# A decoder block in float32 on Trainium2: one tile of a depthwise convolution from TensorE to VectorE, another from VectorE to GpSimd

## The chip, the cores and the metric

The kernel runs on one core of one Trainium2 chip. The metric is the device time of one launch, in microseconds. Five engines take part, each with an instruction queue of its own that it works through in order: TensorE (PE, matmuls), VectorE (DVE), ScalarE (ACT), GpSimd (POOL), and SyncE (SP), which issues the loads and stores.

## The reference

One block with batch 1, 256 tokens, width 2048, all in float32. The convolution is depthwise and causal with 31 taps: each of the 2048 channels has its own taps.

```python
mod = silu(c) @ mod_w + mod_b                       # six vectors of 2048
h = rms_norm(x, norm1_g) * (1 + sc1) + sh1
u = h @ conv_w_in + conv_b_in                       # 2048 -> 4096
a, gt = split(u, 2);  u = a * sigmoid(gt)
u = depthwise_conv(u, conv_dw_w, 31 taps) + conv_dw_b
y = silu(layer_norm(u, ln_g, ln_b)) @ conv_w_out + conv_b_out
x = x + (1 + g1) * y
h = rms_norm(x, norm2_g) * (1 + sc2) + sh2
x = x + (1 + g2) * (square(relu(h @ mlp_w1)) @ mlp_w2)
```

## The kernel before

Activations lie with channels on the 128 partitions: 16 tiles of 128 channels by 256 tokens. The weights are loaded once, one megabyte at a time (128 by 2048), into seven buffers named `raw`.

A float32 product is made of three products of shorter numbers. For each weight block two halves of 128x1024 are prepared. ScalarE copies the **high part** (`hi`, L206), and another engine subtracts it from the weight to get the **low part** (`lo`, L209). Both have six buffers. In the input jobs GpSimd makes the low parts; later it makes some, VectorE the others.

The work is a list of jobs. Job n from 0 to 15 gives tile n of the gated input (`u`): it multiplies h by two weight blocks, one for `a`, one for the gate. Jobs 0 to 7 are done together at the start, while the modulation columns are loaded. Jobs 8 to 15 follow one at a time (`mm`, L234 and L235; in job 15 L230 to L232), then eight output jobs (`out`), then the jobs of the MLP (`up`, `down`).

In the loop over jobs, step n first splits the weights of job n+1 (`splits`), so GpSimd works one job ahead of TensorE. Then come the matmuls of job n, the evacuation (L532, L533) and the gate (L798, L800) that write `u[n]`.

The convolution of the 16 tiles is shared between two engines:

- On **TensorE**, the tiles of `PE_TILES` (`pe_conv`, L783): 32 matmuls with small diagonal blocks. Each tile needs a `diag` of its taps, made by GpSimd (L768), and a `wide` copy of `u`, 16 copies of 32x284 (`copy_wide`, L758 on VectorE and L760 on ScalarE). `CONV_AT` says behind which job's matmuls a tile stands, `COPY_AT` in which step ScalarE makes its copies.
- On **VectorE**, the others (`conv_steps`): one instruction of 128x256 per tap (L666 to L672), sums in PSUM (`acc`), two tiles interleaved. `ADVANCE` says how many taps are issued in step n.

Tile 0 and tile 1 come first, because a shift (an estimate of the mean, `find_shift`, L718) is taken from them. It is added to all tiles ahead of the statistics of the layer norm: tiles below `UNSHIFTED` = 7 get it later (`add_shift`), the others while they are summed.

Between jobs TensorE also multiplies 32 **row chunks** of `mod_w` (`mod_chunk`, L324), four matmuls each. `LATE_IN[n]` says how many follow job n. When a group of 16 is complete, ScalarE copies the sums (`rowsb`, L331) and TensorE folds them (L371). `stats` (L728) sums tiles and squares for the layer norm.

In an output job ScalarE scales the result in two halves (L1006), VectorE adds x (L1007), and the weights of the next job are split meanwhile (L206, L209).

The Tile framework's scheduler puts all this into one order per engine. `tc.issue_after(x)` makes an instruction stand behind x in that order, and `urgent()` raises its priority. The order is fixed when the kernel is built.

Of the kernel before, what the change touches and what calls it, by code (L numbers as in the profile page):

```python
# [8 lines left out]
F32 = mybir.dt.float32  # L9
F32R = mybir.dt.float32r  # L10
AF = mybir.ActivationFunctionType
ALU = mybir.AluOpType
PSUM = bass.MemoryType.PSUM

P = 128
T = 256
D = 2048
KT = D // P
FF = 4 * D
QUARTERS = FF // D  # L20
TAPS = 31
# [18 lines left out]
COLS += [w * KT + k for w in (SH2, G2) for k in range(KT)]  # L40
RAW = 7
FIRST = 4
PE_TILES = (0, 1, 2, 9, 10, 12, 14, 15)
CONV_AT = {9: (0,), 10: (1,), 11: (2,), 12: (9,), 13: (10,), 14: (12,), 15: (14,)}
ADVANCE = {7: 41, 8: 14, 9: 46, 10: 46, 11: 39, 12: 31, 13: 27, 14: 99}
SHIFT = 2
COPY_AT = {8: 0, 9: 1, 10: 2, 11: 9, 12: 10, 13: 12}
PADDING = 720
UNSHIFTED = 7
LATE_IN = [0] * 8 + [4, 4, 4, 4, 4, 2, 0, 10]  # L50
AHEAD = 2
LATE_OUT = [1, 1, 2, 3, 3, 3, 1, 1]
COLS_IN = 1
# [13 lines left out]
def conv_block(ctx: ExitStack, tc: tile.TileContext, x, vec, dwq, c_row, mod_r, mod_c, w_first, w_in, w_out, w1, w2, out):  # L67
    nc = tc.nc
# [12 lines left out]
    nc.scalar.dma_start(v[:, 0:soon], vec[:, 0:soon])  # L81
    dwq_sb = const.tile([P, 32 * len(PE_TILES)], F32, name="dwq_sb")

    def col(name, j=0, n=1):
        at = VEC[name] + j
        return v[:, at : at + n]
# [31 lines left out]
    state = {"used": 0}  # L118
# [12 lines left out]
    def urgent():  # L131
        return tc.high_priority(offset=URGENT)
# [56 lines left out]
    def take(key):  # L189
        assert order[state["used"]] == key, (order[state["used"]], key)  # L190
        state["used"] += 1
        waiting[home(key)] -= 1
        top_up()
        return raw.pop(key)

    def split_w(key, engine):
        w = take(key)
        if key[:2] == ("up", 0) and key[2] < UNSCALED:
            shown[key] = w
        halves = []  # L200
        for h in range(2):
            ks = slice(h * HALF, (h + 1) * HALF)
            hi = wts.tile([P, HALF, P], F32R, name="hi", bufs=6)
            lo = wts.tile([P, HALF, P], F32R, name="lo", bufs=6)
            with tc.issue_after(state["silu"]) if key == ("out", 1, 1) else ExitStack():
                state["w_hi"] = nc.scalar.activation(hi, w[:, ks, :], AF.Copy).ins  # L206
            by = nc.vector if key == ("in", HELD, 0) and h == 0 else engine
            with tc.issue_after(state["e_end"]) if key[0] == "out" and engine is nc.vector else ExitStack():
                end = by.tensor_tensor(lo, w[:, ks, :], hi.bitcast(F32), op=ALU.subtract)  # L209
            if by is nc.gpsimd:  # L210
                state["pool"] = end.ins
            halves.append((hi, lo))
        parts[key] = halves
# [8 lines left out]
    def mm(p, c, key, acts_of, ks=range(KT), merged=False):  # L222
        halves = parts[key]
        for k in ks:
            hi, lo = halves[k // HALF]
            m = acts_of[k // 2][:, k % 2, :]
            if merged:
                out_p, begin, end = p[:, c, 0:T], k == 0, k == KT - 1
                w = hi[:, k % HALF, :]
                nc.tensor.matmul(out_p, w, m[:, 0:T], start=begin, stop=False)  # L230
                nc.tensor.matmul(out_p, w, m[:, T : 2 * T], start=False, stop=False)  # L231
                state["mm_end"] = nc.tensor.matmul(out_p, lo[:, k % HALF, :], m[:, 0:T], start=False, stop=end)  # L232
                continue
            nc.tensor.matmul(p[:, c, :], hi[:, k % HALF, :], m, start=(k == 0), stop=(k == KT - 1))  # L234
            state["mm_end"] = nc.tensor.matmul(  # L235
                p[:, c, T : 2 * T], lo[:, k % HALF, :], m[:, 0:T], start=False, stop=(k == KT - 1),
                skip_group_check=True,
            )
# [204 lines left out]
    def ps_two():  # L443
        return ps.tile([P, 2, T], F32, name="acc", bufs=2)

    def two():
        return tmp.tile([P, 2, T], F32, name="two", bufs=6)
# [40 lines left out]

    quota = {("in", i): n for i, n in enumerate(LATE_IN)}
    quota.update({("out", i): LATE_OUT[i] for i in range(HALF)})  # L490
    after = {}
    for job in jobs:
        n = quota.get(job, 0)
# [3 lines left out]
        if job[:2] in LATE_GATE:  # L497
            n = LATE_GATE[job[:2]][job[2]]
# [22 lines left out]
    def splits(job):  # L521
        for c in range(2):
            if job + (c,) in parts_early:
                continue
            on_pool = job[0] == "in" or job in POOLED
            with urgent():
                split_w(job + (c,), nc.gpsimd if on_pool else nc.vector)

    def evac(p, cs=slice(0, 2), out=None):
        t1 = two()[:, cs, :]  # L530
        t2 = two()[:, cs, :] if out is None else out
        nc.scalar.activation(t1, p[:, cs, T : 2 * T], AF.Copy)  # L532
        nc.vector.tensor_tensor(t2, p[:, cs, 0:T], t1, op=ALU.add)  # L533
        return t2
# [4 lines left out]
    for k2 in range(HALF):  # L539
        s = two()  # L540
# [8 lines left out]
    with urgent():  # L549
        part = two()[:, 0, :]  # L550
# [64 lines left out]
    for k in range(KT):  # L615
# [4 lines left out]
        if c == 0:  # L620
            n = two()
# [7 lines left out]
        if last:  # L629
            w = take(("first", k))  # L630
# [16 lines left out]
    cp = conv_pool.__enter__()  # L647
# [4 lines left out]
    def cv(k):  # L652
        return cvs[k // 4][:, k % 4, :]
# [6 lines left out]
    def tap_of(ct, j):  # L660
        return u[ct][:, j : j + T], col("dww", ct * TAPS + j)
# [21 lines left out]
            yield  # L683
        join(cv(ct), acc[:, 1, :], rest)

    on_dve = [ct for ct in range(KT) if ct not in PE_TILES]

    def stream():
        tail = iter(())
# [18 lines left out]
    def advance(n):  # L708
        for _ in range(n):
            next(conv_taps, None)  # L710
# [40 lines left out]
    def copy_wide(ct, both=True):  # L751
        wides[ct] = cp.tile([P, 4, T + 28], F32, name="wide", bufs=2)
        for q in range(4):
            for g in range(4):
                dst = wides[ct][32 * q : 32 * q + 32, g, :]
                src = u[ct][32 * g : 32 * g + 32, q : q + T + 28]
                if both and (g % 2 or (q, g) == (3, 2)):
                    nc.vector.tensor_copy(dst, src)  # L758
                else:
                    nc.scalar.activation(dst, src, AF.Copy)  # L760
# [3 lines left out]
    def make_diag(ct):  # L764
        diags[ct] = cp.tile([P, 32, 32], F32, name="diag", bufs=2)
        at = PE_TILES.index(ct)
        with tc.issue_after(state["pool"]):
            nc.gpsimd.tensor_tensor(  # L768
                diags[ct],
                col("same", 0, 32)[:, None, :].to_broadcast([P, 32, 32]),  # L770
                dwq_sb[:, 32 * at : 32 * at + 32][:, :, None].to_broadcast([P, 32, 32]),
                op=ALU.mult,
            )
# [22 lines left out]
    def gate(i, t2):  # L796
        sg = two()[:, 0, :]
        state["sg"] = nc.scalar.activation(sg, t2[:, 1, :], AF.Sigmoid, bias=col("b_in", KT + i))  # L798
        u[i] = ubufs[i % len(ubufs)]
        state["gated"] = nc.vector.scalar_tensor_tensor(  # L800
            u[i][:, PAD : PAD + T], t2[:, 0, :], col("b_in", i), sg, op0=ALU.add, op1=ALU.mult
        ).ins
        return sg
# [6 lines left out]
    with urgent():  # L810
        split_w(jobs[HELD] + (0,), nc.gpsimd)
        take(("vec", 0))
        with tc.issue_after(state["w_hi"]):
            gate(0, held[0])
        for i in range(1, 6):
            gate(i, held[i])
        with tc.issue_after(state["sg"].ins):
            split_w(jobs[HELD] + (1,), nc.gpsimd)
        with tc.issue_after(state["w_hi"]):
            gate(6, held[6])  # L820
        gate(7, held[7])
    advance(ADVANCE[HELD - 1])

    for n, job in enumerate(jobs):
        if n < HELD:
            continue
        for ct in CONV_AT.get(n, ()) + ((15,) if n == KT - 1 else ()):
            make_diag(ct)
        if n == KT - 1:
            taken = [(key, take(key)) for key in cols_in]  # L830
        if n < len(jobs) - 1:
            splits(jobs[n + 1])
        if n in COPY_AT:
            with tc.issue_after(state["sg"].ins) if n == HELD else ExitStack():
                copy_wide(COPY_AT[n], False)
        if n == KT - 1:
            for key in parts_early:
                split_w(key, nc.gpsimd)
        kind, i = job[0], job[-1]
# [25 lines left out]
        elif kind == "in":  # L865
            rows = [key for key in after[job] if key not in cols_in] if i < KT - 1 else []
            for c in range(2) if i < KT - 1 else (1, 0):
                for ks in (range(HALF), range(HALF, KT)):
                    with tc.issue_after(state.pop("rows_end")) if "rows_end" in state else ExitStack():
                        mm(p, c, job + (c,), hl, ks, i == KT - 1)  # L870
            if not CONV_AT.get(n):
                with tc.issue_after(state["mm_end"].ins):
# [8 lines left out]
        if kind == "in":  # L881
            with urgent():
                gate(i, evac(p, out=p[:, :, 0:T]) if i < KT - 1 else p[:, :, 0:T])
                if i >= KT - 2:
                    copy_wide(i)
            if n == KT - 4:
                add_shift(cvs[0], 4)
                add_shift(cvs[1][:, 0:3, :], 3)
# [2 lines left out]
            if n == KT - 1:  # L891
                state["e_end"] = add_shift(cvs[3][:, 0:1, :], 1)
                for key, w in taken:
                    mod_col(key[1], w)
            for ct in CONV_AT.get(n, ()):
                with tc.issue_after(state["mm_end"].ins):
# [7 lines left out]
            with tc.issue_after(state["gated"]):  # L904
                advance(ADVANCE.get(n, 0))
            if n == KT - 2:
# [51 lines left out]
            for k2 in range(HALF):  # L958
                e = two()
                if k2 == 0:  # L960
                    with urgent():
                        nc.gpsimd.tensor_tensor(e, pair_of(cvs, 0), spread(mu), op=ALU.subtract)
                        new_hl(0)
                        f = [ps_two()[:, 0, :] for _ in range(2)]
# [10 lines left out]
                f = ps_two()  # L975
# [93 lines left out]
        else:  # L1069
# [13 lines left out]
            for t, cs, p in sums.pop((kind, i // 2)):  # L1083
                at = slice(512 * (i // 2) + cs.start, 512 * (i // 2) + cs.stop)
                s = y[:, t, at]
# [71 lines left out]
```

## Time and profile before

| | |
|---|---|
| median of 3 runs | 1099.27 us (1099.25 to 1099.31) |
| profiled execution | 1099.38 us, of which its span 1097.6 us |
| TensorE busy | 1080.8 us (98%) |
| VectorE busy | 750.3 us (68%) |
| ScalarE busy | 511.0 us (47%) |
| GpSimd busy | 196.0 us (18%) |
| granted TensorE clock | 1.0 in all slices |

The page of the profile has a section of busy times, a picture of the span in 40 slices, the DMA queues, the chain of work that ended last, the costliest groups of instructions, and the DMA issues. In a row, `lo<-raw,hi` says that tile `lo` is written from `raw` and `hi`; `x4` counts instructions; what stands in brackets is the time the engine was idle before it and what ended that. In the profile a float32 matmul of this kernel counts twice, so the 32 matmuls of one tile's convolution are `x64`. All times of rows are microseconds from the start of the span.

### The profile page before, as it was taken

The page shows a single profiled execution, that of the slowest core. Times are in us where ns is not written, and L with a number is a line of the kernel's source. Part 1 is how long each engine was busy: PE and PEld are TensorE (multiplying, and loading weights), DVE is VectorE, ACT ScalarE, POOL GpSimd, SP SyncE. Part 2 cuts the span into 40 slices and gives each one's busy share as a digit, 9 for nine tenths or more (in the row PEclk, how much of TensorE's full clock was granted, in tenths as well). Part 3 has the DMA queues.
Part 4 walks back from the last instruction along what each step waited for, and adds up shares of the span by engine and source line. Part 5 has one row for each costly group of instructions (what it writes and reads, how often), then busy time and mean ns, then how long its engine had stood idle before and what let it go on. Part 6 is the DMA issues. An engine that isn't in the chain of part 4 may idle for free.

```text
span 1097.6 us, 15426 instructions
## 1 busy us (share of the span) xinstructions
PE 1080.8 (98%) x6034; PEld 890.7 (81%) x6034; DVE 750.3 (68%) x1029; ACT 511.0 (47%) x682; POOL 196.0 (18%) x119
## 2 busy tenths in 40 slices
PE   7999999999999999999999999999999999999998
PEld 3888875768599998888888888888888888888887
DVE  5777889998567887678854677545566665565653
ACT  4111396765675586444443444333444333444431
POOL 0000176677589261000000000000000000000000
PEclk9999999999999999999999999999999999999999
DMA  9999998985999976898987889657888777788621
GB/s 384 422 420 421 416 420 340 380 310 198 357 393 402 378 269 225 269 296 306 402 324 213 235 265 322 249 126 296 251 233 248 226 211 211 230 250 241 208 67 39
DMA packets 142315, 314.23 MB, mean 286 GB/s; under 512 B 87585, under 2 KB 105505, under 8 KB 107297
## 3 DMA queue, kind: packets, MB, share of 16 engines
q1 hardware_dynamic: 142096, 313.11, 81.2%
q8 instruction: 47, 0.77, 0.3%
q14 instruction: 26, 0.21, 0.1%
q10 hardware_dynamic: 146, 0.13, 0.0%
HBM read 301.15 MB, written 12.07 MB: 285 GB/s over the span
## 4 chain that ended last, share of the span: by engine, by line
PE 85%; DMA 12%; DVE 2%; ACT 1%; POOL 0%; issue 0%; SPq 0%
PE mm L272 20%; PE mm L271 20%; PE mm L273 20%; DMA raw<-mod_c 9%; PE mm L234 6%; PE mm L235 3%; PE acc L231 2%; PE acc L230 2%; PE acc L232 2%; PE mm L783 2%; PE row L324 2%; DMA raw<-mod_r 1%; DMA raw<-w_in 1%; DVE raw L404 1%; DMA x<-x 1%; PE mm L230 0%
## 5 line engine op out<-in xcount | busy, mean ns | idle before, releaser
L206 ACT ACTIVATE hi<-raw 128x1024 fp32r<-128x1024 f32 x320 | 335.6, 1058 | 358.7 <-PE mm L273 320.9
L209 DVE TENSOR_TENSOR lo<-raw,hi 128x1024 fp32r<-128x1024 f32 x257 | 311.8, 1219 | 176.2 <-ACT hi L206 174.2
L272 PE MATMUL mm<-lo,u 128*128 128x512 f32 x496 | 193.0, 389 | 0.0
L271 PE MATMUL mm<-hi,u 128*128 128x512 f32 x496 | 193.0, 389 | 0.0
L273 PE MATMUL mm<-hi,u 128*128 128x512 f32 x496 | 192.9, 389 | 0.0
L273 PE MATMUL mm<-hi,hl 128*128 128x512 f32 x480 | 186.7, 389 | 0.0
L272 PE MATMUL mm<-lo,hl 128*128 128x512 f32 x480 | 186.7, 389 | 0.0
L271 PE MATMUL mm<-hi,hl 128*128 128x512 f32 x480 | 186.7, 389 | 0.0
L209 POOL TENSOR_TENSOR lo<-raw,hi 128x1024 fp32r<-128x1024 f32 x63 | 155.3, 2493 | 61.1 <-ACT hi L206 61.1
L404 DVE SCALAR_TENSOR_TENSOR raw<-raw,cond 128x2048 f32<-128x2048 f32 x50 | 116.6, 2333 | 45.5 <-DMA raw<-mod_c 45.5
L273 PEld LDWEIGHTS mm<-hi,u 128*128 128x128 f32 x496 | 93.1, 188 | 19.3
L272 PEld LDWEIGHTS mm<-lo,u 128*128 128x128 f32 x496 | 93.1, 188 | 19.0
L271 PEld LDWEIGHTS mm<-hi,u 128*128 128x128 f32 x496 | 93.1, 188 | 19.0
L273 PEld LDWEIGHTS mm<-hi,hl 128*128 128x128 f32 x480 | 90.1, 188 | 18.7
L271 PEld LDWEIGHTS mm<-hi,hl 128*128 128x128 f32 x480 | 90.1, 188 | 18.7
L272 PEld LDWEIGHTS mm<-lo,hl 128*128 128x128 f32 x480 | 90.1, 188 | 18.7
L672 DVE SCALAR_TENSOR_TENSOR acc<-u,v,acc 128x256 f32<-128x256 f32 x224 | 96.7, 483 | 2.2
L234 PE MATMUL mm<-hl,hi 128*128 128x512 f32 x224 | 80.1, 401 | 0.0
L576 PE MATMUL mm<-two,first 128*128 128x256 f32 x240 | 56.5, 390 | 8.1 <-ACT two L634 8.1
L230 PE MATMUL acc<-hl,hi 128*128 128x256 f32 x224 | 63.4, 283 | 0.0
L231 PE MATMUL acc<-hl,hi 128*128 128x256 f32 x224 | 63.4, 283 | 0.0
L232 PE MATMUL acc<-hl,lo 128*128 128x256 f32 x224 | 63.4, 283 | 0.0
(212 smaller groups left out, 1262.8 us busy)
## 6 DMA issues: line engine op xcount, KB each, us to landing
raw<-w SPq DMA_DIRECT2D x128, 1024.0 KB, 5.5
raw<-mod_c SPq DMA_DIRECT2D x62, 1024.0 KB, 11.2
raw<-mod_r SPq DMA_DIRECT2D x32, 1024.0 KB, 7.9
raw<-w_in SPq DMA_DIRECT2D x16, 1024.0 KB, 10.6
raw<-w_out SPq DMA_DIRECT2D x16, 1024.0 KB, 8.5
first<-w_first SPq DMA_DIRECT2D x15, 1024.0 KB, 19.8
flat<-two SPq DMA_DIRECT2D x30, 256.0 KB, 2.6
two<-flat SPq DMA_DIRECT2D x120, 64.0 KB, 4.2
```

What stands on the lines that cost most here:

```text
L206: state["w_hi"] = nc.scalar.activation(hi, w[:, ks, :], AF.Copy).ins
L209: end = by.tensor_tensor(lo, w[:, ks, :], hi.bitcast(F32), op=ALU.subtract)
L230: nc.tensor.matmul(out_p, w, m[:, 0:T], start=begin, stop=False)
L231: nc.tensor.matmul(out_p, w, m[:, T : 2 * T], start=False, stop=False)
L232: state["mm_end"] = nc.tensor.matmul(out_p, lo[:, k % HALF, :], m[:, 0:T], start=False, stop=end)
L234: nc.tensor.matmul(p[:, c, :], hi[:, k % HALF, :], m, start=(k == 0), stop=(k == KT - 1))
L271: nc.tensor.matmul(p, p_hi, hi, start=begin, stop=False)
L272: nc.tensor.matmul(p, p_hi, lo, start=False, stop=False)
L273: nc.tensor.matmul(p, p_lo, hi, start=False, stop=end)
L404: nc.vector.scalar_tensor_tensor(w, w, 1.0, cb, op0=ALU.mult, op1=ALU.mult, accum_out=acc)
L576: step = nc.tensor.matmul(held[n][:, c, :], w[:, 2 * n + c, :], h, start=k == 0 and c == 0, stop=k == KT - 1, skip_group_check=True)
L672: nc.vector.scalar_tensor_tensor(out, s, w, acc, op0=ALU.mult, op1=ALU.add)
```

## The change

Tile 2 leaves `PE_TILES` and joins VectorE's stream. Tile 7 leaves VectorE's stream and goes to GpSimd (`pool_stream`): the first tap is one instruction with the bias, each of the other 30 taps is a multiplication by the tap's column into `part` and an addition to the tile, and an addition of the shift ends it. The 32 steps are issued in groups of 6, 7, 7, 7 and 5 in the steps 8 to 12. Each group stands behind the last low part for the next job, and the low parts of the job after that stand behind the group.

With one tile less on TensorE, tiles 9 and 10 move one job earlier, and job 13 has no convolution. One row chunk moves from job 8 to job 11. The `wide` copies of tile 14 are all made by ScalarE (nine of its 16 were VectorE's), those of tile 15 are shared as before, and the other copies and the groups of VectorE's taps are moved to suit.

```diff
-PE_TILES = (0, 1, 2, 9, 10, 12, 14, 15)
-CONV_AT = {9: (0,), 10: (1,), 11: (2,), 12: (9,), 13: (10,), 14: (12,), 15: (14,)}
-ADVANCE = {7: 41, 8: 14, 9: 46, 10: 46, 11: 39, 12: 31, 13: 27, 14: 99}
+PE_TILES = (0, 1, 9, 10, 12, 14, 15)
+CONV_AT = {9: (0,), 10: (1,), 11: (9,), 12: (10,), 14: (12,), 15: (14,)}
+POOL_TILE = 7
+POOL_TAPS = {8: 6, 9: 7, 10: 7, 11: 7, 12: 5}
+ADVANCE = {7: 41, 8: 10, 9: 45, 10: 45, 11: 38, 12: 24, 13: 24, 14: 99}
-COPY_AT = {8: 0, 9: 1, 10: 2, 11: 9, 12: 10, 13: 12}
+COPY_AT = {8: 0, 9: 1, 10: 9, 11: 10, 13: 12}
-LATE_IN = [0] * 8 + [4, 4, 4, 4, 4, 2, 0, 10]
+LATE_IN = [0] * 8 + [3, 4, 4, 5, 4, 2, 0, 10]
...
             with tc.issue_after(state["e_end"]) if key[0] == "out" and engine is nc.vector else ExitStack():
-                end = by.tensor_tensor(lo, w[:, ks, :], hi.bitcast(F32), op=ALU.subtract)
+                with tc.issue_after(state["pool_tap"]) if key[0] == "in" and "pool_tap" in state else ExitStack():
+                    end = by.tensor_tensor(lo, w[:, ks, :], hi.bitcast(F32), op=ALU.subtract)
...
-    on_dve = [ct for ct in range(KT) if ct not in PE_TILES]
+    on_dve = [ct for ct in range(KT) if ct not in PE_TILES and ct != POOL_TILE]
+
+    def pool_stream():
+        out = cv(POOL_TILE)
+        s, w = tap_of(POOL_TILE, 0)
+        yield nc.gpsimd.tensor_scalar(out, s, w, col("dwb", POOL_TILE), op0=ALU.mult, op1=ALU.add)
+        for j in range(1, TAPS):
+            s, w = tap_of(POOL_TILE, j)
+            f = cp.tile([P, T], F32, name="part", bufs=2)
+            nc.gpsimd.tensor_scalar(f, s, w, None, op0=ALU.mult)
+            yield nc.gpsimd.tensor_tensor(out, out, f, op=ALU.add)
+        yield nc.gpsimd.tensor_tensor(out, out, state["shift"], op=ALU.add)
+
+    pool_taps = pool_stream()
...
         if n < len(jobs) - 1:
             splits(jobs[n + 1])
+        for _ in range(POOL_TAPS.get(n, 0)):
+            with urgent(), tc.issue_after(state["pool"]):
+                state["pool_tap"] = next(pool_taps).ins
...
-                    copy_wide(i)
+                    copy_wide(i, i == KT - 1)
```

## The prediction

> **What bounds the kernel now.** I read the page first: the span, the busy shares and the chain that ended last.
>
> ```profile
> span 1097.6 us, 15426 instructions
> ...
> PE 1080.8 (98%) x6034; PEld 890.7 (81%) x6034; DVE 750.3 (68%) x1029; ACT 511.0 (47%) x682; POOL 196.0 (18%) x119
> ...
> PE 85%; DMA 12%; DVE 2%; ACT 1%; POOL 0%; issue 0%; SPq 0%
> ```
>
> TensorE is the bound: 98% busy, 85% of the chain. The 12% of DMA lies in the opening. GpSimd (POOL) looks idle at 18%, but that is an average. Next I asked for the busy time by stage, cut at the starts of the input jobs 10 to 14 (the columns after the length are busy time and instruction count of each engine, then clock, DMA share and GB/s).
>
> ```profile
> 171.00:192.00 21.00, 21.00 (x168) 13.54 (x166) 21.00 (x55) 14.71 (x29) 12.36 (x6) 1.00 0.93 352
> 192.00:210.40 18.40, 18.40 (x161) 12.69 (x161) 17.53 (x42) 11.97 (x22) 13.18 (x6) 1.00 0.92 357
> 210.40:229.80 19.40, 19.40 (x173) 13.79 (x169) 19.33 (x50) 13.87 (x26) 12.44 (x7) 1.00 0.85 332
> 229.80:246.60 16.80, 16.80 (x145) 12.28 (x145) 16.24 (x38) 11.81 (x22) 11.14 (x6) 1.00 0.88 353
> 246.60:262.90 16.30, 16.30 (x148) 12.46 (x148) 14.66 (x31) 6.38 (x9) 13.84 (x7) 1.00 0.68 260
> ```
>
> TensorE has no gap in any of them, and the clock is full. VectorE (third number) is full too, so it can't take a tile more. GpSimd (fifth) works 11 to 14 of 16 to 21 us: 5 to 9 us of most jobs are free. The timeline of GpSimd shows where they lie.
>
> ```profile
> 150.91 4.72 POOL L209 TENSOR_TENSOR lo<-raw,hi 128x1024 fp32r<-128x1024 f32 x2 [0.31 <-ACT hi L206]
> 155.59 1.92 POOL L768 TENSOR_TENSOR diag<-v,dwq_sb 128x1024 f32<-128x1024 f32 x1
> ...
> 178.33 9.43 POOL L209 TENSOR_TENSOR lo<-raw,hi 128x1024 fp32r<-128x1024 f32 x4 [6.27 <-ACT hi L206]
> 187.71 1.92 POOL L768 TENSOR_TENSOR diag<-v,dwq_sb 128x1024 f32<-128x1024 f32 x1
> ```
>
> A low part costs 2.35 us from start to start ((187.71 - 178.33) / 4), and rows overlap by 0.05 (178.33 + 9.43 = 187.76), so a diag costs 1.87. The parts for the job that begins at 192.0 are done at 187.7, the first of them at 180.7: GpSimd is some 11 us ahead of TensorE. Free time and lead together decide this case.
>
> **What the change takes from TensorE.** These rows are of the chain in order of time, and the last is of TensorE's timeline.
>
> ```profile
> 241.29 3.59 PE mm L783 x64
> ...
> 246.60 0.43 PE mm L234
> ...
> 258.10 3.59 PE mm L783 x64
> 261.69 1.28 PE small L728 x20
> ```
> ```profile
> 151.43 1.06 PE L324 MATMUL row<-raw,cz 128*32 128x512 f32 x8 [0.85 <-DMA raw<-mod_r]
> ```
>
> One tile's 32 matmuls go: -3.59 us, all on the path. Job 13 is the one that ends without a convolution. The row chunk that leaves job 8 is the one that ended in a 0.85 us wait for its load: -0.85. Its own matmuls reappear after job 11, so they count nothing. The loads stand in the queue of SyncE in the order of use, so the chunk's load falls behind three pairs of `w_in` loads, which all come one megabyte sooner: 0.
>
> The built order shows a cost, too: with five chunks after job 11 the four fold matmuls (L371) stand behind the first matmul of job 12, where 41 stood ahead of them before. They need ScalarE's copy of the row sums, 0.60 us (L331, in the next fence), which starts when the last row matmul is done. One matmul, at most 0.43 us, covers part of it, and the hand-overs come on top: I take +0.45, from 0 to 0.6.
>
> **A stall far from the change.** The scheduler also reorders ScalarE in the output stage. Rows of ScalarE, then of VectorE, before:
>
> ```profile
> 216.93 0.60 ACT L331 ACTIVATE rowsb<-row 128x512 f32<-128x512 f32 x1
> ...
> 233.97 2.24 ACT L760 ACTIVATE wide<-u 32x284 f32<-32x284 f32 x5
> ...
> 371.04 1.99 ACT L206 ACTIVATE hi<-raw 128x1024 fp32r<-128x1024 f32 x2
> 378.69 1.11 ACT L1006 ACTIVATE acc<-acc,gb,modc 128x256 f32<-128x256 f32 x2 [5.66 <-PE acc L232]
> ```
> ```profile
> 374.35 2.36 DVE L209 TENSOR_TENSOR lo<-raw,hi 128x1024 fp32r<-128x1024 f32 x2
> ```
>
> At 371.04 ScalarE splits the first weights of the last output job, 7 us before the job ahead of it ends and its L1006 starts (378.69). In the built order after the change these two splits stand between the two halves of that L1006, and ScalarE takes its queue in order. The first L1006 can't start before TensorE has ended the job ahead, so TensorE then has no weights: it waits for half of L1006 (1.11 / 2) and a high part (1.99 / 2), some 1.6 us, and then for VectorE's low part (2.36 / 2), of which the high matmuls fill a little. Sum +2.6 us. I bound it by 2.0 (0.6 filled or overlapped) and 2.9 (hand-overs on top); nothing hides it, since TensorE has no other matmul in its queue there. It does not depend on the taps.
>
> Without GpSimd's part the sum is -3.59 - 0.85 + 0.45 + 2.6 = -1.4 us.
>
> **What it costs on GpSimd.** 31 taps become 31 multiplications and 30 additions, all of 128x256, and one addition of the shift: 31 pairs. The trace has no multiplication by a column on GpSimd. The nearest rows (an addition of the same size, its shortest, median and longest in ns; runs of additions that each wait for the one before; a subtraction of 128x512; writes alone):
>
> ```profile
> L1014 POOL TENSOR_TENSOR sqacc<-sqacc,two x12: 740/747/2672, 334.5 to 383.8; 128x256 f32<-128x256 f32 x12
> ```
> ```profile
> 287.34 0.53 POOL L940 MEMSET shz<- 128x512 f32 x1 [7.89 <-ACT two L794]
> ...
> 291.64 8.97 POOL L977 TENSOR_TENSOR two<-cv,mu 128x512 f32<-128x512 f32 x7
> ...
> 357.82 2.38 POOL L1014 TENSOR_TENSOR sqacc<-sqacc,two 128x256 f32<-128x256 f32 x3
> ...
> 382.38 4.13 POOL L1014 TENSOR_TENSOR sqacc<-sqacc,two 128x256 f32<-128x256 f32 x2 [11.00 <-ACT two L1009]
> ```
>
> Addition: (2.38 - 0.74) / 2 = 0.82 us from start to start with the wait for the one before. Every pair has one such wait, and the multiplication overlaps by 0.05. So a pair costs the multiplication's length m + 0.77. Bounds of m: writes alone take 0.53 for 512 elements, so half of that, 0.27; the addition, which reads two operands, 0.74. From 1.28 (8.97 / 7) and 2.35 us for 512 and 1024 the subtraction costs 0.20 us plus 2.1 ns per element; with one operand to read instead of two I halve the slope: 0.20 + 256 x 1.05 ns = 0.47. With something for the scalar column I take m = 0.50, near the middle of the bounds: 1.27 us a pair (1.04 to 1.51).
>
> [...]
>
> How much room is there? The taps of job n stand behind the four low parts for job n+1, the next low parts behind the taps, and the diag among the taps. From 150.91, which the change leaves where it is, GpSimd then has no more idle time. Up to the end of the diag of tile 12 it has 24 low parts (56.4 us), that diag and four others (9.4) and the 31 pairs. TensorE comes to that convolution at 258.10 - 3.59 - 0.85 + 0.45 + 1.28 (the 1.28 us of L728, which the new order puts ahead of it) = 255.4. Room: 255.4 - 150.9 - 56.4 - 9.4 = 38.7 us, or **1.25 us a pair**. The first low part of job 14 (19 low parts, four diags; needed one matmul, 0.4, after 246.60 - 3.99 = 242.6) allows 243.0 - 150.9 - 44.7 - 7.5 = 39.9, or 1.29. Above 1.25 every 0.1 us a pair is 3.1 us of TensorE, at this place and, with 1.35 and more, at the starts of jobs 13, 12 and 11 as well, for the same queue is late there. Behind a late tap wait the low parts, then TensorE; ScalarE's next high parts wait too, for a buffer that GpSimd still reads, and with them the evacuation behind them.
>
> At 1.27 the excess is 0.02 x 31 = 0.6 us. **Sum: 1099.38 (the profiled execution; its span 1097.6 and 1.8 around it; the median of the runs is 1099.27) - 1.4 + 0.6 = 1098.6 us.**
>
> **Costed at nothing.** VectorE keeps eight tiles (2 comes, 7 goes) of 31 taps; covered by the same order, but it has no spare time, so a tap more would show. ScalarE loses 16 `wide` copies of 0.45 us (2.24 / 5) and takes the nine of tile 14 that VectorE had; the 16 now take 7.2 us from the gate of job 14 on, under the 11 us of job 15's matmuls. If the cover failed, convolution 14 would be late by what is missing.
>
> **Rivals.** *GpSimd becomes the bound (slower).* If m is above 0.59, the queue sets the starts of jobs 12 to 14. For: no idle time is left by construction, and the addition at 0.74 shows what such an instruction may cost. Against: one operand fewer. At m = 0.66 a pair is 1.43, the excess 0.18 x 31 = 5.6, the time 1103.6; at 0.74 it is 1106.1. It decides from a pair of 1.36 on (1101.5).
>
> *GpSimd and VectorE collide (slower).* The two additions at 382.38 took 4.13 us beside these VectorE rows, the three at 357.82 only 2.38:
>
> ```profile
> 357.63 1.20 DVE L400 SCALAR_TENSOR_TENSOR raw<-raw,mm 128x1024 f32<-128x1024 f32 x1
> ...
> 383.08 2.83 DVE L404 SCALAR_TENSOR_TENSOR raw<-raw,cond 128x2048 f32<-128x2048 f32 x1
> ```
>
> L404 reads two operands from SBUF, L400 one there and one (`mm`) in PSUM. VectorE's taps are of the second kind (`acc` is in PSUM), and the low parts beside them keep 2.35 us; so the taps should not collide. If they did, by the 0.45 us that some additions take longer (1.18 for 0.74), it would be 14 us: 1112.6. [...]
>
> *The stall in the output stage does not come (faster).* For: nothing in the diff asks for it. Against: the queue is in order. With the taps in time it gives 1099.38 - 4.0 = 1095.4.
>
> **How the numbers follow.** About 0.2%, 2.2 us, is what a measurement of this kernel can tell from no change: 1097.1 to 1101.5. Forecast (m up to 0.59): 0.55. GpSimd as the bound: 0.32. Collision: 0.03. No stall: 0.10. So faster 0.10, same 0.55, slower 0.35. The likeliest case alone reaches from 1097.2 (pairs under 1.25, and one of stall and fold at its low bound) to 1101.5; the range reaches on to m = 0.69 (1104.5) and leaves out what lies above and the missing stall.
>
> **What would show it.** Right: GpSimd without a gap from 151 to some 262 us; a multiplication near 0.50 us; TensorE with gaps of about 0.5 us at L371, together under 1.5 us ahead of the convolution of tile 12 and of job 14, 2.6 us at the last output job, and none at jobs 10 to 12. Wrong: multiplications of 0.6 us and more, with waits of TensorE for `lo` at the starts of jobs 12 and 13; additions of 1.2 us; or no gap near 375 us.

## The result, and the profile after

The changed kernel takes **1133.16 us** (median of 6 runs: 1123.8 and 1124.0 in two, 1133.0 to 1135.3 in four), the kernel before 1099.30: a ratio of 1.028 (1.024 to 1.033). It is 34 us slower, where 1098.6 and no change was forecast, and it lies above the range. The profiled execution is one of the shorter ones, 1124.01 us.

First TensorE's busy time and its waits (in a row: total, times, longest):

```profile
span 1122.2 us, 15331 instructions
PE 1094.0 (97%) x5970; PEld 896.9 (80%) x5970; DVE 744.7 (66%) x1020; ACT 508.4 (45%) x674; POOL 241.7 (22%) x180
```
```profile
PE mm L238 <- POOL lo L212: 8.8, 4, 3.5
...
PE acc L233 <- ACT hi L208: 1.6, 1, 1.6
PE acc L799 <- DVE wide L774: 1.2, 1, 1.2
PE acc L235 <- DVE lo L212: 0.8, 1, 0.8
PE acc L799 <- ACT wide L776: 0.7, 1, 0.7
...
PE row L374 <- ACT rowsb L334: 0.3, 1, 0.3
```

Line numbers are those of the changed kernel: L212 makes the low parts (L209 before), L698 and L699 are the two halves of a pair, L774 and L776 the `wide` copies on VectorE and ScalarE, L407 is L404. The forecast stall stands there (1.6 and 0.8 us at the last output job), and the fold's 0.3. What was not forecast are four waits for `lo`, 8.8 us, at the starts of jobs 11 to 14. GpSimd's own rows give the reason:

```profile
180.52 0.92 POOL L698 TENSOR_SCALAR part<-u,v 128x256 f32<-128x256 f32 x1
181.41 0.73 POOL L699 TENSOR_TENSOR cv<-cv,part 128x256 f32<-128x256 f32 x1
182.24 0.92 POOL L698 TENSOR_SCALAR part<-u,v 128x256 f32<-128x256 f32 x1
```

A multiplication takes 0.92 us, more than the addition, and a pair 182.24 - 180.52 = 1.72 us.

Two more readings. TensorE has 64 matmul records fewer and yet is busy 1094.0 us instead of 1080.8. Part of it is a lower clock around the waits. The first two rows are 170 to 189 us; the last two are the 3.4 us behind the wait of job 11:

```profile
L237 PE MATMUL mm<-hl,hi 128*128 128x512 f32 x30 | 10.6, 399 | 0.0
L238 PE MATMUL mm<-hl,lo 128*128 128x256 f32 x31 | 8.7, 281 | 0.0
```
```profile
L237 PE MATMUL mm<-hl,hi 128*128 128x512 f32 x5 | 3.1, 629 | 0.0
L238 PE MATMUL mm<-hl,lo 128*128 128x256 f32 x6 | 2.5, 417 | 1.7 <-POOL lo L212 1.7
```

The granted clock was 1.00 in all of these windows before; now it is 0.93, 0.92 and 0.85 in three of them (window, its length, TensorE's busy time and instructions, the clock, the DMA share, GB/s):

```profile
190.00:213.00 23.00, 21.32 (x170) 0.93 0.69 268
213.00:235.00 22.00, 20.89 (x168) 0.92 0.77 309
235.00:251.00 16.00, 13.19 (x84) 1.00 0.93 377
251.00:274.00 23.00, 19.48 (x164) 0.85 0.64 229
```

By windows of 0.1 us the granted clock was 0.50 from about 192.4 to 195.8, from 216.3 to 219.7, and for twice that time from 253.8 to 260.7. The length of a wait alone doesn't tell where: waits of 1.7 us at job 11 and of 0.8 at job 12 (0.3 for the fold shortly before) had such a stretch behind them, and the 2.8 us at job 13 had no slow matmul behind them:

```profile
238.49 0.39 PE L238 MATMUL mm<-hl,lo 128*128 128x256 f32 x1 [2.81 <-POOL lo L212]
238.72 0.39 PE L237 MATMUL mm<-hl,hi 128*128 128x512 f32 x1
```

The slow stretches begin 23.9 and 37.6 us apart, 7 and 11 times the 3.41 us that the first one took. So it seems that where a wait falls counts beside its length; no run varied that alone. An estimate from these windows, busy time times (1 - clock), puts the cost at 6.0 us of TensorE's time.

Another part lies in a stage that the change does not touch. These are matmuls of the MLP, before and after:

```profile
L271 PE MATMUL mm<-hi,u 128*128 128x512 f32 x496 | 193.0, 389 | 0.0
```
```profile
L274 PE MATMUL mm<-hi,u 128*128 128x512 f32 x496 | 195.8, 395 | 0.0
```

Three such lines, 1488 matmuls; from start to start they are 232.4 ns apart instead of 226.8: 8.4 us. Those that read `hl` instead of `u2` kept their 389 ns. The granted clock in these windows is 1.00. Less the 3.7 us of the convolution that has gone, 6.0 and 8.4 leave 2.5 us of the busy time unplaced.

By place, in this execution, TensorE is 13.2 us late at the first output matmul (308.32 for 295.10), 16.1 at the last matmul of the output jobs (405.97 for 389.88), and 24.6 at the end: the MLP adds 8.5.

### The profile page after: what moved, and what is told of

Same layout as the page of the kernel before. It is cut to its first block, busy times and chain, and to the rows that moved or that the text cites. A ratio compares the mean times of both kernels' runs of the same rounds, so it can differ in the third digit from the quotient of the medians.

```text
span 1122.2 us, 15331 instructions
## 1 busy us (share of the span) xinstructions
PE 1094.0 (97%) x5970; PEld 896.9 (80%) x5970; DVE 744.7 (66%) x1020; ACT 508.4 (45%) x674; POOL 241.7 (22%) x180
## 4 chain that ended last, share of the span: by engine, by line
PE 73%; DVE 2%; ACT 2%; issue 0%; DVEq 0%; ACTq 0%
PE mm L275 20%; PE mm L274 20%; PE mm L276 20%; PE acc L235 2%; PE acc L234 2%; PE acc L233 2%; PE mm L237 2%; PE mm L238 1%; ACT wide L776 1%; DVE wide L774 0%; DVE acc L675 0%; PE acc L799 0%; PE acc L276 0%; PE acc L275 0%; PE acc L274 0%; DVE raw L407 0%
## 5 line engine op out<-in xcount | busy, mean ns | idle before, releaser
L212 DVE TENSOR_TENSOR lo<-raw,hi 128x1024 fp32r<-128x1024 f32 x257 | 312.7, 1221 | 197.6 <-ACT hi L208 197.0
L274 PE MATMUL mm<-hi,u 128*128 128x512 f32 x496 | 195.8, 395 | 0.0
L275 PE MATMUL mm<-lo,u 128*128 128x512 f32 x496 | 195.7, 395 | 0.0
L276 PE MATMUL mm<-hi,u 128*128 128x512 f32 x496 | 195.7, 395 | 0.0
L212 POOL TENSOR_TENSOR lo<-raw,hi 128x1024 fp32r<-128x1024 f32 x63 | 155.2, 2493 | 27.6 <-ACT hi L208 27.6
L407 DVE SCALAR_TENSOR_TENSOR raw<-raw,cond 128x2048 f32<-128x2048 f32 x50 | 118.0, 2362 | 40.7 <-DMA raw<-mod_c 40.7
L675 DVE SCALAR_TENSOR_TENSOR acc<-u,v,acc 128x256 f32<-128x256 f32 x224 | 93.9, 481 | 1.2
L237 PE MATMUL mm<-hl,hi 128*128 128x512 f32 x224 | 84.9, 419 | 0.0
L238 PE MATMUL mm<-hl,lo 128*128 128x256 f32 x224 | 65.7, 293 | 8.8 <-POOL lo L212 8.8
L233 PE MATMUL acc<-hl,hi 128*128 128x256 f32 x224 | 63.5, 283 | 1.6 <-ACT hi L208 1.6
```

The source lines that it names most:

```text
L238: state["mm_end"] = nc.tensor.matmul(p[:, c, T : 2 * T], lo[:, k % HALF, :], m[:, 0:T], start=False, stop=(k == KT - 1), skip_group_check= ...
L274: nc.tensor.matmul(p, p_hi, hi, start=begin, stop=False)
L275: nc.tensor.matmul(p, p_hi, lo, start=False, stop=False)
L276: nc.tensor.matmul(p, p_lo, hi, start=False, stop=end)
L407: nc.vector.scalar_tensor_tensor(w, w, 1.0, cb, op0=ALU.mult, op1=ALU.mult, accum_out=acc)
L675: nc.vector.scalar_tensor_tensor(out, s, w, acc, op0=ALU.mult, op1=ALU.add)
```

## The experiments

**The MLP.** `PE_TILES` has one entry less, and with it the table `dwq_sb` has 224 columns instead of 256. Everything allocated behind it moves by 128 bytes, `hi`, `lo` and `hl` among it; `u2`, on the other side of SBUF, does not.

```diff
-    dwq_sb = const.tile([P, 32 * len(PE_TILES)], F32, name="dwq_sb")
+    dwq_sb = const.tile([P, 32 * 8], F32, name="dwq_sb")
...
-                    state["load"] = nc.sync.dma_start(dwq_sb, dwq)
+                    state["load"] = nc.sync.dma_start(dwq_sb[:, 0 : 32 * len(PE_TILES)], dwq)
```

> The changed kernel with the table of taps for TensorE (dwq_sb) kept at 256 columns instead of 224; the last 32 are not used. Nothing else differs, but every SBUF tile behind the table lies 128 bytes higher again, as before the change, while u2, on the other side of SBUF, stays. Theory (address): the 1488 matmuls of the MLP that read u2 took 395 ns each after the change and 389 before; they return to 389, and the last stretch from the first MLP matmul to the end is shorter by some 8.2 us (1488 x 5.5 ns): about 1116 us where the change gave 1124, 1125 where it gave 1133. Rival (a lower clock as a consequence of the stalls, or some other late effect of GpSimd's queue): the matmuls stay at 395 ns and the time between 1124 and 1135.

Measured: 1116.9 us (1115.4 to 1118.0), ratio 1.016 (1.015 to 1.018). That is 7.1 us below the short runs of the change (1124.0), and 8.6 between the two profiled executions; why none of the four is as long as the long ones is told below. The matmuls are back at 389 ns:

```profile
L274 PE MATMUL mm<-hi,u 128*128 128x512 f32 x496 | 193.1, 389 | 0.0
```

The other way round, in the kernel before:

```diff
-PADDING = 720
+PADDING = 688
```

> The kernel before with PADDING = 688 instead of 720: u2 lies 128 bytes higher relative to hi and lo, the same distance as in the changed kernel. No instruction differs. Theory (address): the MLP matmuls that read u2 take 395 ns instead of 389, and the time is 1099.3 + 8.2 = 1107.5 us. Rival: the distance does not matter, 1099.3 us and 389 ns.

Measured: 1107.78 us, ratio 1.0077 (1.0062 to 1.0092), 8.5 us more with only addresses moved:

```profile
L271 PE MATMUL mm<-hi,u 128*128 128x512 f32 x496 | 195.8, 395 | 0.0
```

So the distance between `u2` and the weights costs some 8.5 us, and it is shown in both directions. How much of a distance does harm?

> The kernel before with PADDING = 592 instead of 720: u2 lies 512 bytes higher. In the kernel before u2 lies a multiple of 4096 bytes from hi and lo (193696 - 74912 = 29 x 4096); 128 bytes more cost 8.5 us. Theory (only a multiple of 4096 is good): 395 ns for the matmuls that read u2, some 1107.7 us. Rival (a multiple of 512 is enough): 389 ns and 1099.3 us.

Measured: 1099.08 us in the one run, 389 ns. So 512 bytes more than the distance of the kernel before cost nothing, and 128 bytes more cost 8.5 us. What lies between wasn't tried.

**Without the pairs.** `pool_stream` yields only its first tap and the addition of the shift.

> The run with the 256-column table, and with the 30 pairs of multiplication and addition of tile 7 left out (the first tap and the addition of the shift stay; tile 7 lacks its other taps). ScalarE's order in the output stage is that of the kernel before here, so the stall there goes too. Theory (GpSimd's queue is what costs the conv stage): no wait of TensorE for lo in jobs 11 to 14, and the prediction's sum without GpSimd and without the stall: 1099.4 - 3.59 - 0.85 + 0.45 = 1095.4 us. Rival (VectorE's stream with tile 2 instead of 7, or the wide copies, is late as well): waits remain ahead of the convolutions, and the time is 1098 us or more.

Measured: 1097.09 us (10 runs), ratio 0.998 (0.997 to 0.999). No wait for `lo` is left, but there is one for the copies of tile 15:

```profile
PE acc L798 <- DVE wide L773: 1.2, 1, 1.2
```
```profile
273.54 7.05 DVE L773 COPY wide<-u 32x284 f32<-32x284 f32 x9
```
```profile
266.65 11.53 POOL L212 TENSOR_TENSOR lo<-raw,hi 128x1024 fp32r<-128x1024 f32 x4 [2.50 <-ACT hi L208]
```

Nine copies took 7.05 us, two of them 2.4 each beside GpSimd's last low parts and the rest 0.3; in the kernel before it was 4.40 us for nine. So of the 1.7 us that the sum lacks against 1095.4, 1.2 are this wait; 0.5 I can't place.

**The length of a multiplication.** 40 GpSimd instructions in the kernel before, whose results are not used.

> The kernel before with 40 further GpSimd instructions of 128x256 issued in an MLP job, where GpSimd is otherwise idle; their results are not used. In groups of four: multiplication by a column, source at an even offset; the same, source one element on; multiplication by a column and addition of a column in one instruction, both offsets; multiplication by a column and addition of 0.0; multiplication by a constant; addition of two tiles; multiplication of two with one operand repeated along the row; a copy; and four alternating pairs as in the change. In the changed kernel the first tap (two operations, even offset) took 0.56 us and the 30 multiplications (one operation, offsets of both kinds) 0.92. Theory (form): one operation costs 0.92 at both offsets and two operations 0.56 at both. Rival 1 (offset): 0.56 at the even offset and 0.92 at the odd one, whatever the form. Rival 2 (the neighbourhood in the conv stage): every multiplication takes some 0.5 us here. The kernel's time stays at 1099.3 us.

Measured (min/median/max in ns). In order: column, even and odd source; two columns, even and odd; column and 0.0; constant; addition of tiles; repeated operand; copy.

```profile
L829 POOL TENSOR_SCALAR pad<-pad,v x4: 925/926/928, 301.4 to 304.4; 128x256 f32<-128x256 f32 x4
L831 POOL TENSOR_SCALAR pad<-pad,v x4: 922/927/932, 305.4 to 322.5; 128x256 f32<-128x256 f32 x4
L833 POOL TENSOR_SCALAR pad<-pad,v x4: 545/766/984, 331.7 to 358.1; 128x256 f32<-128x256 f32 x4
L835 POOL TENSOR_SCALAR pad<-pad,v x4: 562/570/3631, 362.2 to 369.9; 128x256 f32<-128x256 f32 x4
L837 POOL TENSOR_SCALAR pad<-pad,v x4: 476/487/790, 371.2 to 373.2; 128x256 f32<-128x256 f32 x4
L839 POOL TENSOR_SCALAR pad<-pad x4: 847/850/1909, 373.8 to 379.4; 128x256 f32<-128x256 f32 x4
L841 POOL TENSOR_TENSOR pad<-pad x4: 642/1500/2569, 380.3 to 384.2; 128x256 f32<-128x256 f32 x4
...
L845 POOL COPY pad<-pad x4: 393/400/2457, 394.0 to 398.0; 128x256 f32<-128x256 f32 x4
```

It is the form: with one operation 0.92 at both offsets, with two 0.55, and with an addition of 0.0 as the second 0.48. Both rivals, the offset and the neighbourhood, fall. The time did not stay: 1108.3 us, since the instructions were scheduled earlier than meant, into the output stage, where TensorE waited 7.1 us for `sqacc`, which queued behind them, and some of each four took longer (up to 3.63 us); so the shortest of each four is read.

So the change can be had with the shorter form (and the wide table, as in all runs from here on but one):

```diff
-            nc.gpsimd.tensor_scalar(f, s, w, None, op0=ALU.mult)
+            nc.gpsimd.tensor_scalar(f, s, w, 0.0, op0=ALU.mult, op1=ALU.add)
```

> The run with the 256-column table, and the multiplication of each pair with a second operation, an addition of 0.0 (the result is the same). Alone such an instruction took 0.48 us instead of 0.925. ScalarE's order in the output stage is that of the kernel before here. Theory (the length of the multiplication sets the queue): a pair takes 0.48 + 0.77 = 1.25 us, which is the room; no waits for lo beyond 0.5 us, and the time is that without pairs, 1097.1, up to 1098. Rival (GpSimd shares something with VectorE in the conv stage, so that pairs stay longer than their parts): pairs of 1.4 us and more, waits for lo ahead of jobs 12 to 14, 1102 us or more.

Measured: 1100.62 us (11 runs, 1099.8 to 1102.3), ratio 1.0011 (1.0002 to 1.0020); the profiled execution 1099.86. That is 2.6 us above the end of the expectation. The pair is 161.16 - 159.87 = 1.29 us, no wait for `lo` is left, and two others are:

```profile
159.87 0.48 POOL L698 TENSOR_SCALAR part<-u,v 128x256 f32<-128x256 f32 x1
160.31 0.75 POOL L699 TENSOR_TENSOR cv<-cv,part 128x256 f32<-128x256 f32 x1
161.16 0.48 POOL L698 TENSOR_SCALAR part<-u,v 128x256 f32<-128x256 f32 x1
```
```profile
PE row L374 <- ACT rowsb L334: 1.9, 1, 1.9
PE acc L799 <- DVE wide L774: 1.8, 1, 1.8
```

Of the 16.3 us that this takes away, (1.72 - 1.29) x 31 = 13.3 are the pairs and 2.4 the stall, which this order does not have. A middle length, with a second operation by a column of ones:

> The run with the 256-column table, and the multiplication of each pair with a second operation by a column, a multiplication by 1.0 (the result is the same). Alone an instruction with two columns took 0.55 to 0.57 us. ScalarE's order in the output stage is that of the change, with the stall. Theory: a pair of 0.56 + 0.77 = 1.33 us, 0.08 above the room; 31 x 0.08 = 2.5 us on top of 1097.1, and 2.4 to 2.9 for the stall: 1102 to 1102.5. Rival (each wait also lowers the clock, which makes it dearer than the queue alone): 1104 us or more.

Measured: 1110.81 us, ratio 1.0105 (1.0091 to 1.0118); more than the theory gives. The multiplication is 0.56 as expected, the pair 1.37, and there is one wait of 1.7 us for `lo`. The larger part is a wait of 6.5 us for the copies of tile 15, with this on VectorE:

```profile
272.14 11.11 DVE L407 SCALAR_TENSOR_TENSOR raw<-raw,cond 128x2048 f32<-128x2048 f32 x1
```

The rival is right in part. Behind both waits the granted clock was 0.51, from 245.9 to 249.3 us and from 288.8 to 293.7 (over 245 to 260, 275 to 290 and 290 to 305 us it was 0.89, 0.89 and 0.88), and the convolution of tile 15 took 5.99 us, where it took 3.66 in the kernel before:

```profile
288.86 5.99 PE L799 MATMUL acc<-wide,diag 128*32 128x256 f32 x64 [6.47 <-ACT wide L776]
```

The same estimate as above gives 4.1 us for the lower clock. With it the parts add up: 1097.1 + 1.7 + (6.5 - 1.2, the wait that the run without pairs has too) + 2.4 (stall) + 0.4 (a wait for a load) + 4.1 = 1111.0, measured 1110.8.

**The column product.** That instruction took 2.28 us before. It explains also why the changed kernel has two times; one run more of it, unaltered:

> The changed kernel once more, nothing altered, on the chip of the other runs. It gave 1123.8 and 1124.0 in two runs and 1133.0 to 1135.3 in four, with mean granted clocks of 0.993 and 0.986; the run with the 256-column table gave 1115.4 to 1118.0 at 0.992 to 0.994. Theory (the address adds 8.4 us and nothing else): 1123.8 to 1126.4. Rival (the address also lowers the clock in some runs): 1133 again in part of them, at 0.986.

Measured: 1133.6, 1132.9, 1124.0 and 1133.4 us. The profiled one is long. Its VectorE, GpSimd and wait:

```profile
280.00 13.99 DVE L407 SCALAR_TENSOR_TENSOR raw<-raw,cond 128x2048 f32<-128x2048 f32 x1
```
```profile
280.54 1.91 POOL L784 TENSOR_TENSOR diag<-v,dwq_sb 128x1024 f32<-128x1024 f32 x1
282.41 9.43 POOL L212 TENSOR_TENSOR lo<-raw,hi 128x1024 fp32r<-128x1024 f32 x4
```
```profile
PE acc L799 <- ACT wide L776: 10.9, 1, 10.9
```

The short run of the change, and the kernel before:

```profile
280.55 3.77 DVE L407 SCALAR_TENSOR_TENSOR raw<-raw,cond 128x2048 f32<-128x2048 f32 x1
```
```profile
282.15 11.51 POOL L212 TENSOR_TENSOR lo<-raw,hi 128x1024 fp32r<-128x1024 f32 x4
```
```profile
270.20 2.28 DVE L404 SCALAR_TENSOR_TENSOR raw<-raw,cond 128x2048 f32<-128x2048 f32 x1
```

L407 reads two operands from SBUF. In the long run it stands on VectorE from 280.00 to 293.99, and GpSimd's back-to-back instructions end at 282.41 + 9.43 = 291.84, 2.15 us before it does: it seems to have done its work of 2.28 us only when GpSimd stopped. The product of 11.11 us above ended 2.15 us after GpSimd's queue, too (at 283.25 and 281.10). In the short run it got in behind the diag: the first of the four low parts took 4.43 us instead of 2.4. Why it gets in in one run and not in another isn't shown. Ten taps, the gate of tile 15 and its copies queue behind it on VectorE. The wait is 10.9 us instead of 1.2 and 0.7, 9.0 more, and the two groups of runs lie 9.4 us apart (1124.0 and 1133.4 in the middle). In the run with the wide table the product took 3.87 in the profiled execution, the shortest of the four. In the kernel before, GpSimd was idle for 1.52 us just then:

```profile
271.21 8.23 POOL L209 TENSOR_TENSOR lo<-raw,hi 128x1024 fp32r<-128x1024 f32 x3 [1.52 <-ACT hi L206]
```

Removing the stall in the output stage was to show its price, and ran into the same:

```diff
+            if key == ("out", HALF - 1, 0):
+                state["last_hi"] = state["w_hi"]
...
+                    with tc.issue_after(state["last_hi"]) if i == HALF - 2 else ExitStack():
+                        nc.scalar.activation(t2[:, c, :], t2[:, c, :], AF.Identity, ...)
```

> The run with the 256-column table, with ScalarE's order in the output stage put back: the two halves of the seventh job's L1025 stand behind both high parts of the last job's first weights. Nothing else moves. Theory (the stall is 1.6 + 0.8 us of waits): no wait for hi or lo near 391 us, and the time is 2.4 to 2.9 us below the run with the 256-column table alone (1116.9): 1114.0 to 1114.5. Rival (the wait comes back later, since the matmuls behind it run into their own inputs sooner): 1116 us or more.

Measured: 1121.69 us, ratio 1.0205 (1.0191 to 1.0219): 4.8 us more, against both. The waits for `hi` and `lo` at the last output job are gone as expected; the four runs lie within 0.6 us, and in the profiled one the product was held up for 15.56 us, until 2.14 us after GpSimd's queue. So the price of the stall was not measured by this run. The product moved out of the way:

```diff
+                shifted, state["e_end"] = state["e_end"], state["copied"]
                 for key, w in taken:
                     mod_col(key[1], w)
+                state["e_end"] = shifted
```

(`state["copied"]` is the last of VectorE's copies of tile 15.)

> The run with ScalarE's order put back (1121.7 us, where VectorE's column product L409, 128x2048 with two operands from SBUF, took 15.56 us and TensorE waited 10.9 us for the wide copies of tile 15), with that one VectorE instruction moved behind VectorE's copies of tile 15. It then runs when GpSimd's queue is empty. Theory (VectorE's instruction cannot start while GpSimd runs one instruction after the other, and VectorE's taps, the gate of tile 15 and its copies queue behind it): the instruction takes 2.3 us, the wait ahead of the convolution of tile 15 falls from 10.9 to some 2 us, and the time to 1121.7 - 9 = 1112.7 us. Rival (the product is long because its data or its clock are slow, not because of GpSimd): it takes 10 us or more at the new place too. Second rival (the wait for the copies has another cause): the wait stays at 10 us.

Measured: 1114.98 us, ratio 1.015 (1.013 to 1.016), 6.7 less, where 9 were expected. The product takes 2.29 us, and the wait for the copies is 1.0:

```profile
294.72 2.29 DVE L409 SCALAR_TENSOR_TENSOR raw<-raw,cond 128x2048 f32<-128x2048 f32 x1
```
```profile
PE mm L240 <- POOL lo L214: 9.2, 4, 3.0
...
PE row L329 <- DMA raw<-mod_r: 1.7, 1, 1.7
PE acc L237 <- DVE lo L214: 1.6, 1, 1.6
PE acc L801 <- DVE wide L776: 1.0, 1, 1.0
```

That is 9.9 us of waits less, and two new ones, 1.7 and 1.6: 6.6 in sum. That it meets the measured 6.7 so closely is partly luck: the other waits and the lower clock change by about 1 us each, in both directions. Both rivals fall.

**A version that beats both?** Two attempts on the shorter form; of the three edits of the first, the spread of the taps is shown.

```diff
-POOL_TAPS = {8: 6, 9: 7, 10: 7, 11: 7, 12: 5}
+POOL_TAPS = {8: 6, 9: 6, 10: 6, 11: 6, 12: 6, 13: 2}
```

> The run with the multiplication that also adds 0.0 (1100.6 us), with the column product moved behind the copies of tile 15, the taps on GpSimd spread as 6, 6, 6, 6, 6 and 2 over the steps 8 to 13 instead of 6, 7, 7, 7 and 5, and ScalarE's high parts kept ahead of L1025 in the output jobs 3 to 6. It had a wait of 1.9 us for rowsb, because GpSimd still held the buffers that the next weights needed, and one of 1.8 us for the copies of tile 15. Theory: the first goes, the second stays (GpSimd's last low parts lie beside the copies): 1100.6 - 1.9 = 1098.7 us. At best, if both go, 1097. Rival: two taps in step 13 make the low parts of job 15 late, and TensorE waits there: 1100 us or more.

Measured: 1100.00 us (11 runs, 1099.7 to 1100.2), ratio 1.0007 (0.9998 to 1.0016). The wait for `rowsb` went to 0.3, but a low part of VectorE is now late in the output stage, 1.7 us. With the spread of the taps alone:

> The run with the multiplication that also adds 0.0 (1100.6 us), with one edit only: the taps on GpSimd in groups of 6, 6, 6, 6, 6 and 2 over the steps 8 to 13 instead of 6, 7, 7, 7 and 5. The run with three mends lost its wait for rowsb by this spread, but its other edits brought a wait of 1.7 us for a low part of VectorE in the output stage. Theory: without those edits that wait does not come, the wait for rowsb stays away, and what is left are the copies of tile 15: 1100.0 - 1.7 = 1098.3 us, 1 us below the kernel before. Rival (the column product stands among GpSimd's last instructions again and is held up there, as in the run that took 15.56 us for it): 1105 us or more in part of the runs.

Measured: 1100.81 us (11 runs, 1099.1 to 1105.2), ratio 1.0021 (1.0011 to 1.0031); two of the runs took 1104.7 and 1105.2, as the rival has it, but neither was profiled. The product took 2.90 us in the profiled one, the nine copies 8.52, and TensorE waited 2.5 us for them. No version tried beats the kernel before; a combination of the two was not run.

## Why the prediction was wrong

*The length of the multiplication (the step that failed).* m was taken 0.50 between bounds of 0.27 and 0.74 and measured 0.92. The upper bound was the error: it let the count of operands decide, and the form decided. The case "GpSimd becomes the bound" came, beyond its dearest price. The rest of that step held. A pair was m + 0.77: 1.72 for 0.92, 1.37 for 0.56, 1.29 for 0.48, so m + 0.8. The room was 1.25 us: (1.72 - 1.25) x 31 = 14.6 us above the run without pairs is 1111.7, and the run with the product moved has 1115.0, of which 3.3 are its two new waits. The lower clock needs no term of its own in this sum: while GpSimd sets the pace, a slower TensorE only waits less. In the short run of the change the waits for `lo` are 8.8 us and the lower clock is 6.0 by the estimate above, together 14.8. Behind a wait that is not the queue's it comes on top: the convolution of tile 15 took 3.66 us in the kernel before, 5.99 in the run with the column of ones and 5.70 in the long run of the change. The prediction has no term for that.

The estimate of 0.47 us, from the rows with half the slope for one operand, came near the form with 0.0 (0.48) and lies above the copy (0.39); the multiplication alone (0.92) took about twice as long.

*The output stage.* 2.6 was forecast, 1.6 + 0.8 = 2.4 came; also, the order that makes it depends on small things: it came in some of these kernels and not in others.

*TensorE's tile, the row chunk, the fold.* -4.0 was forecast, and the run without pairs is 2.2 us below the kernel before. Of the difference, 1.2 us are the copies of tile 15, costed at nothing, where the prediction named as cover only the copies of tile 14.

*GpSimd and VectorE collide (0.03).* The prediction weighed the taps and the additions, and those do not collide: the additions kept 0.73. But it had L404 itself as the instruction beside which two additions took 4.13 us, and did not ask where else one stands: there was one at 270 us, beside the end of GpSimd's queue, where "no idle time is left". The product reads two operands from SBUF; the copies of tile 15, which read one, stood up to 2.4 us instead of 0.30 as well, so it is not shown that two operands are the condition. The traces show what happened: in three profiled executions the VectorE instruction stood until GpSimd paused, 2.28 us becoming 11.1, 14.0 and 15.6; in others it got in, for 2.9 to 4.0 us, and a GpSimd instruction took longer instead (4.43 us for 2.4 in the short run of the change). What decides between the two stays open.

*What was not in it at all.* 128 bytes of a table, 8.5 us.

The sum by the runs, for the long times: 1097.1 + 14.6 (pairs) + 2.4 (output stage) + 8.5 (address) + 0.7 + 9.0 (copies of tile 15: 0.7 more than without pairs, then the product) = 1132.3, and 1134.3 with the lower clock behind the last wait (5.70 - 3.66 = 2.0); measured 1133.4 in the middle of the long runs. Without the product 1123.3, measured 1123.8 and 1124.0.

## What to carry to other kernels

Price an instruction by its own form on its engine, not by one with more operands: here a second, idle operation made it half as long (0.48 us for 0.92). Before an engine's last idle time is filled, look for what lives on that idle time elsewhere: in three profiled executions a VectorE instruction with two SBUF operands stood until GpSimd paused (11.1, 14.0 and 15.6 us for 2.28), with everything queued behind it. When an edit changes the size of any SBUF tile, compare the durations of the matmuls in stages that it does not touch (here 395 ns for 389 after 128 bytes), and keep the addresses.

## What the hardware showed that was not expected

- GpSimd, 128x256 in float32: a multiplication by a column 0.92 us, by a constant 0.85, by a column with an addition of a column 0.55 to 0.57, with an addition of 0.0 0.48; an addition of two tiles 0.63 at its shortest, 0.72 to 0.76 in the change; a copy 0.39.
- A VectorE instruction of 2.28 us with two SBUF operands stood 11.1, 14.0 and 15.6 us beside a GpSimd queue without pauses, each time until 2.14 or 2.15 us after the end of that queue; a copy of 0.30 us stood 2.4.
- A matmul whose stationary operand lies 128 bytes off the distance that the kernel before has to its weights comes 232.4 ns after the one before instead of 226.8, 2.5% more, at a granted clock of 1.00; 512 bytes off cost nothing in one run.
- A wait of 1.7 us was followed by 3.4 us at a granted clock of 0.50, in which matmuls took 629 ns instead of 399; one of 2.8 us in the same execution was not.
